# Two transformer blocks on one core: differential attention's TensorE order written out by slots of 12 products, and weights' low parts made by adding transfers

## The chip, the core and the metric

The kernel runs on one core of a Trainium2 chip. The core has five engines with an instruction queue each, which is worked off in order: TensorE (matmuls, PE in the rows, its weight loads PEld), VectorE (DVE), ScalarE (ACT), GpSimd (POOL) and SyncE (SP, which here only issues transfers). The metric is the device time of one execution in microseconds (us); the median of several executions counts.

## The reference

Two transformer blocks run one after the other on a sequence of 1024 tokens of width 1024, all in float32. The change touches one stage of the second block, differential attention, with the products that stand beside it:

```python
proj = rms_norm(x) @ w_in                       # d_q, d_k, d_v, c_val, c_gate, m_diff, m_conv, ...
for h in range(8):                              # heads: two score maps each, head width 64, values 128
    s[t] = q[h, t] @ k[h, t].T * 64 ** -0.5     # t = 0, 1; masked by chunks of 64 tokens
    pd = softmax(s[0]) - lam * softmax(s[1])
    o[h] = rms_norm(pd @ v[h], g) * (1 - lambda_init)
y_diff = sigmoid(m_diff) * o
u = c_val * sigmoid(c_gate)                     # convolution module: causal, depthwise, 31 taps
u = depthwise_conv(u, conv_dw)
```

## The kernel before

Activations lie with channels on the 128 partitions and the 1024 tokens along the free axis, in two halves of 512. A float32 product is made of three products in a rounded format (fp32r): every operand is split into a high part and the rest, its low part, and `mm3` adds high by high, high by low and low by high. So one output tile of 128 x 512 over 1024 input channels is 8 x 3 = 24 matmuls (`pdn` in the rows, line 396). A weight block of 128 x 1024 is loaded to `raw` by SP, ScalarE rounds it to `whi` (line 378), and in this stage GpSimd computes `wlo = raw - whi` (line 379, `w_conv` with `w_eng = nc.gpsimd`). For other weights the kernel has another way, `split_dma`: ScalarE writes `whi` and then `-whi` to the low part's place, and a transfer issued by GpSimd adds `raw` to it (lines 384 to 386).

The stage is the function `diff`. For each of the 8 heads, `qkv` makes keys (dk), queries (dq) and values (dv) by dense products; transfers copy the halves of k and swap those of q (`qa<-swp` is the last of that swap); `scores(qb)` makes two score maps for a block of 128 queries (`psc`), VectorE takes the row maxima (`nm`), ScalarE the exponentials (`e`), VectorE joins the two maps (line 1136); `trans` transposes them on TensorE (`ptr`), ScalarE and VectorE split them (`th`, `tl`); `pv` multiplies by the values (`po`). `finish` normalizes a head's output: `colsum` on TensorE (`pst`), a chain of short VectorE operations on 8 columns (`ms`, `rv`, `rr`, `rt`, with a root on ScalarE), a broadcast `bc`, four transposes per half (`prow`), and the products on VectorE. Beside the heads' steps, dense products for the gate (md), and for the convolution's inputs of the next head (cg, cv) fill TensorE. The convolution itself is 31 steps over a tile of 128 x 1024 for each head: one on ScalarE and 30 on VectorE (`cacc`, line 1042). They are given to the scheduler in twos and threes with a priority lowered by `LATER` = 400, to run when VectorE has nothing else.

In this stage a scheduler (of the tile framework) orders all engines, by priorities and by its own estimate of when an operand is ready. The order it makes is fixed when the program is built. On the chip each queue is worked off in that order, and an instruction that waits holds up all that stand behind it on its engine. PSUM, where TensorE writes, is given out in three pools: `psA` (2 score maps), `psB` (2 banks for `pdn`, `po`, `pst`) and `psT` (2 banks for transposes).

Of the kernel before, what the change touches and what calls it, by code (L numbers as in the profile page):

```python
# [50 lines left out]
CS = (2, 3)  # L51
# [8 lines left out]
LATE_AT = ("dk", 0)  # L60
# [225 lines left out]
class Net:  # L286
# [6 lines left out]
    def setup(self, ctx):  # L293
# [30 lines left out]
        self.w_eng = None  # L324
        self.ahead = 1
# [663 lines left out]
    def diff(self, hl, st, pre):  # L989
        nc, tc = self.nc, self.tc  # L990
# [18 lines left out]
        def dense(key, half, w):  # L1009
            ps = self.psB.tile([P, H], F32, tag="B", name="pdn")  # L1010
            self.proj_half(ps, w, hl, half)
            return ps

        def fills(h):

            st_ = {}
            cw = lambda k: self.v("conv_dw", k * CT + h)

            def fill(key, half):
                hs = slice(half * H, half * H + H)  # L1020
                if h == 0:
                    ps = pre.fills[key, half]
                else:
                    if half == 0:
                        st_[key] = self.w_next(f"{key}{h}")
                    ps = dense(key, half, st_[key])
                if key == "cg":
                    if half == 0:
                        st_["sg"] = op.tile([P, S], F32, tag="sg", name="csg")
                    nc.scalar.activation(st_["sg"][:, hs], ps, AF.Sigmoid)  # L1030
                elif key == "cv":
                    if half == 0:
                        st_["u"] = cp.tile([P, 30 + S], F32, tag="u", name="cu", bufs=2)
                        nc.gpsimd.memset(st_["u"][:, 0:30], 0.0)
                    nc.vector.tensor_tensor(st_["u"][:, 30 + half * H:30 + half * H + H],
                                            ps, st_["sg"][:, hs], op=ALU.mult)
                    if half == 1:
                        u = st_["u"]
                        acc = cp.tile([P, S], F32, tag="acc", name="cacc", bufs=1)
                        conv.append(lambda: nc.scalar.activation(acc, u[:, 30:30 + S], AF.Copy, scale=cw(30)))  # L1040
                        for k in range(30):
                            conv.append(lambda k=k: nc.vector.scalar_tensor_tensor(  # L1042
                                acc, u[:, k:k + S], cw(k), acc, op0=ALU.mult, op1=ALU.add))
                        conv.append(lambda: nc.gpsimd.dma_start(self.cvd[h], acc))
                else:
                    if half == 0:
                        st_["sig"] = op.tile([P, S], F32, tag="sig", name="sig")
                    nc.scalar.activation(st_["sig"][:, hs], ps, AF.Sigmoid)

            return st_, {k: [lambda k=k, x=x: fill(k, x) for x in range(2)] for k in ("cg", "cv", "md")}  # L1050

        def gates(i):

            x = []

            def f(half):
                if half == 0:
                    x.extend((self.w_next(f"mc{i}"),
                              cp.tile([P, 30 + S], F32, tag="u", name="mcu", bufs=2)[:, 0:S] if i % 2 else
                              op.tile([P, S], F32, tag="sg", name="mcs")))  # L1060
                w, t = x
                nc.scalar.activation(t[:, half * H:half * H + H], dense("mc", half, w), AF.Sigmoid)
                if half:
                    nc.sync.dma_start(self.sgd[i], t)

            return [lambda: f(0), lambda: f(1)]

        def ktiles():
            return [qp.tile([P, S], F32R, tag=t, name=t) for t in ("k0h", "k0l", "k1h", "k1l")]

        def qkv(h, late):

            k0h, k0l, k1h, k1l = k0 if h == 0 else ktiles()
            a = qp.tile([P, S], F32R, tag="qa", name="qa")
            b = qp.tile([P, S], F32R, tag="qb", name="qb")
            vf = op.tile([P, S], F32, tag="sg", name="vf")
            for key in ("dk", "dq", "dv"):
                w = pre.w[key] if (key, h) == ("dk", 0) else self.w_next(f"{key}{h}")
                for half in range(2):
                    if (key, h, half) == ("dk", 0, 0):  # L1080
                        continue
                    hs = slice(half * H, half * H + H)
                    ps = dense(key, half, w)
                    if key == "dk":
                        self.split(k0h[:, hs], k0l[:, hs], ps)
                    elif key == "dq":
                        nc.scalar.activation(a[:, hs], ps, AF.Copy, scale=0.125)
                        nc.vector.scalar_tensor_tensor(b[:, hs], ps, 0.125, a[:, hs].bitcast(F32),  # L1088
                                                       op0=ALU.mult, op1=ALU.subtract)
                    else:  # L1090
                        nc.scalar.copy(vf[:, hs], ps)
                    if h or key != "dk":
                        conv_steps(CS[0])
                    if (key, half) == LATE_AT:
                        for f in late:
                            f()
                if key == "dk":
                    for src, dst in ((k0h, k1h), (k0l, k1l)):
                        sf, df = src.bitcast(F32), dst.bitcast(F32)
                        nc.sync.dma_start(df[0:64, :], sf[64:128, :])  # L1100
                        nc.sync.dma_start(df[64:128, :], sf[64:128, :])
                        nc.sync.dma_start(sf[64:128, :], sf[0:64, :])
                elif key == "dq":
                    tmp = ep.tile([P, S], F32, tag="e0", name="swp")
                    swap_q(a, b, tmp)
            vh = qp.tile([P, 8, P], F32R, tag="vh", name="vh")
            vl = qp.tile([P, 8, P], F32R, tag="vl", name="vl")
            for c in range(2):
                pt = self.psT.tile([P, 4, P], F32, tag="T", name="pvt")
                for t in range(4):  # L1110
                    nc.tensor.transpose(pt[:, t, :], vf[:, (4 * c + t) * P:(4 * c + t + 1) * P], self.ident)
                self.split(vh[:, 4 * c:4 * c + 4, :], vl[:, 4 * c:4 * c + 4, :], pt)
            return (a, b), ((k0h, k0l), (k1h, k1l)), (vh, vl)

        def scores(qb, q, k, fac):
# [22 lines left out]
            return es[0]  # L1138

        def trans(qb, p, pts):  # L1140
            b = qb % 2
            n = qb + 1
            bs = slice(b * P, (b + 1) * P)
            for c in range(0, n, 4):
                w = min(4, n - c)
                ps = self.psT.tile([P, 4, P], F32, tag="T", name="ptr")
                for k in range(w):
                    nc.tensor.transpose(ps[:, k, :], p[:, (c + k) * P:(c + k + 1) * P], self.ident)
                if pts.get((c // 4)) is None:
                    pts[c // 4] = (tp.tile([P, 4, 256], F32R, tag="th", name="th", bufs=3),  # L1150
                                   tp.tile([P, 4, 256], F32R, tag="tl", name="tl", bufs=3))
                th, tl = pts[c // 4]
                self.split(th[:, 0:w, bs], tl[:, 0:w, bs], ps[:, 0:w, :])

        def pv(i, pts, v, o):
            po = self.psB.tile([P, H], F32, tag="B", name="po")
            n = 2 * i + 2
            for k in range(n):
                th, tl = pts[k // 4]
                cs = slice(P, 256) if k == n - 1 else slice(0, 256)  # L1160
                for a, m in ((v[0], th), (v[0], tl), (v[1], th)):
                    first = k == 0 and a is v[0] and m is th
                    last = k == n - 1 and a is v[1]
                    nc.tensor.matmul(po[:, cs], a[:, k, :], m[:, k % 4, cs], start=first, stop=last,
                                     skip_group_check=True)
            nc.scalar.copy(o[:, i * 256:(i + 1) * 256], po[:, 0:256])

        def finish(h, o, sig, fac):
            pst = self.psB.tile([P, H], F32, tag="B", name="pst")
# [1689 lines left out]
```

## Time and profile before

| | |
|---|---|
| median of 3 runs | 3594.99 us (3591.3 to 3597.71) |
| the profiled execution: own time, span | 3603.38 us, 3601.6 us |
| the stage looked at: from 1360 to 2172 us of the span | 812 us |
| mean granted TensorE clock, whole span | 0.96 of full |

Times on a row are microseconds from the start of the span, unless marked ns. "Idle before, releaser" is the time in which an engine stood still before an instruction, and the instruction whose end let it go on. A matmul's own duration holds the pipeline's filling; what counts for the rate is the distance between two starts.

### The profile page before, as it was taken

The page shows a single profiled execution, that of the slowest core. Times are in us where ns is not written, and L with a number is a line of the kernel's source. Part 1 is how long each engine was busy: PE and PEld are TensorE (multiplying, and loading weights), DVE is VectorE, ACT ScalarE, POOL GpSimd, SP SyncE. Part 2 cuts the span into 40 slices and gives each one's busy share as a digit, 9 for nine tenths or more (in the row PEclk, how much of TensorE's full clock was granted, in tenths as well). Part 3 has the DMA queues.
Part 4 walks back from the last instruction along what each step waited for, and adds up shares of the span by engine and source line. Part 5 has one row for each costly group of instructions (what it writes and reads, how often), then busy time and mean ns, then how long its engine had stood idle before and what let it go on. Part 6 is the DMA issues. An engine that isn't in the chain of part 4 may idle for free. (4 is left out here: it accounts for less than half of the span.)

```text
span 3601.6 us, 42275 instructions
## 1 busy us (share of the span) xinstructions
PE 3326.7 (92%) x15494; PEld 2722.3 (76%) x15494; DVE 2485.1 (69%) x3102; ACT 1673.1 (46%) x2783; POOL 1709.3 (47%) x1147
## 2 busy tenths in 40 slices
PE   8788997999998988999999999999999989999996
PEld 6668885788877776777787886777777768888775
DVE  7888838776767788888877765766477672222777
ACT  5447823444445644444444453535533233333564
POOL 3435207999952342111111126876544187776224
PEclk9889998999999989999999999999999999999998
DMA  3131231222258842222222222333455412222974
GB/s 111 38 105 51 59 117 40 86 83 83 81 178 201 208 114 73 68 73 62 68 68 66 62 67 87 130 129 117 167 202 193 146 54 87 81 83 90 273 175 109
DMA packets 127808, 386.31 MB, mean 107 GB/s; under 512 B 16016, under 2 KB 16272, under 8 KB 127600
## 3 DMA queue, kind: packets, MB, share of 16 engines
q1 hardware_dynamic: 92144, 297.58, 25.3%
q0 software_dynamic: 28400, 61.12, 8.1%
q10 hardware_dynamic: 7056, 24.91, 1.8%
q8 instruction: 122, 2.00, 0.2%
q14 instruction: 86, 0.70, 0.1%
HBM read 232.25 MB, written 84.97 MB: 88 GB/s over the span
## 5 line engine op out<-in xcount | busy, mean ns | idle before, releaser
L379 POOL TENSOR_TENSOR wlo<-raw,whi 128x512 fp32r<-128x512 f32 (+1 forms) x266 | 478.0, 1808 | 788.8 <-ACT whi L378 771.9
L396 PE MATMUL pdn<-h,whi 128*128 128x512 f32 x1664 | 534.4, 402 | 16.8 <-DVE qb L1088 7.3
L1542 DVE TENSOR_TENSOR f<-pf,f 128x512 f32<-128x512 f32 x224 | 154.0, 688 | 363.2 <-PE pf L396 362.7
L378 ACT CAST whi<-raw 128x512 fp32r<-128x512 f32 (+1 forms) x283 | 206.7, 753 | 387.9 <-PE pf L396 169.1
L396 PEld LDWEIGHTS pdn<-h,whi 128*128 128x128 f32 x1664 | 314.6, 193 | 83.1 <-DVE qb L1088 10.2
L1042 DVE SCALAR_TENSOR_TENSOR cacc<-cu,vec,cacc 128x1024 f32<-128x1024 f32 x240 | 357.9, 1491 | 9.8 <-issue 2.2
L396 PE MATMUL pdn<-h,wlo 128*128 128x512 f32 x832 | 331.4, 398 | 0.0
L396 PE MATMUL pd<-whi 128*128 128x512 f32 x644 | 257.8, 400 | 22.1 <-DVE f L1542 10.8
L396 PE MATMUL pd<-whi,wlo 128*128 128x512 f32 x644 | 258.8, 402 | 14.6 <-DMA wlo<-fs 10.2
L396 PE MATMUL pd<-wlo,whi 128*128 128x512 f32 x644 | 256.2, 398 | 0.0
L378 ACT CAST whi<-sb 128x512 fp32r<-128x512 f32 x128 | 79.1, 620 | 342.2 <-PE pf L396 253.7
L379 POOL TENSOR_TENSOR wlo<-sb,whi 128x512 fp32r<-128x512 f32 x128 | 174.3, 1366 | 108.7 <-ACT whi L378 108.5
L379 POOL TENSOR_TENSOR wlo<-sa,whi 128x1024 fp32r<-128x1024 f32 x64 | 178.4, 2788 | 55.5 <-ACT whi L378 55.3
L396 PE MATMUL pf<-h,whi 128*128 128x512 f32 x576 | 183.8, 401 | 10.6 <-ACT a L2469 5.6
L396 PEld LDWEIGHTS pdn<-h,wlo 128*128 128x128 f32 x832 | 160.2, 193 | 33.9
L396 PE MATMUL pp<-h,whi 128*128 128x512 f32 x448 | 149.3, 413 | 24.3 <-ACT h L532 10.1
L386 POOL DMA_DIRECT2D wlo<-fs x92 | 79.9, 871 | 192.8 <-ACT wlo L385 138.8
L396 PEld LDWEIGHTS pd<-whi 128*128 128x128 f32 x644 | 124.2, 193 | 51.5 <-ACT acc L1875 7.9
L396 PEld LDWEIGHTS pd<-whi,wlo 128*128 128x128 f32 x644 | 124.3, 193 | 50.5 <-DMA wlo<-fs 15.9
L396 PEld LDWEIGHTS pd<-wlo,whi 128*128 128x128 f32 x644 | 124.1, 193 | 26.2
L396 PEld LDWEIGHTS pf<-h,whi 128*128 128x128 f32 x576 | 109.4, 192 | 37.9 <-ACT a L2469 6.0
L1542 DVE TENSOR_TENSOR g<-pf,g 128x512 f32<-128x512 f32 x93 | 63.4, 686 | 105.4 <-PE pf L396 89.6
(563 smaller groups left out, 9576.8 us busy)
## 6 DMA issues: line engine op xcount, KB each, us to landing
raw<-in_w_in_dram SPq DMA_DIRECT2D x102, 512.0 KB, 3.5
raw<-in_w_up_dram SPq DMA_DIRECT2D x48, 512.0 KB, 3.5
gd<-f ACTq DMA_DIRECT2D x46, 512.0 KB, 2.6
fs<-gd SPq DMA_DIRECT2D x46, 512.0 KB, 7.0
wlo<-fs POOLq DMA_DIRECT2D x92, 256.0 KB, 5.0
raw<-in_w_ffn_in_dram SPq DMA_DIRECT2D x44, 512.0 KB, 3.5
wlo<-s POOLq DMA_DIRECT2D x69, 256.0 KB, 3.9
fs<-in_w_down_dram SPq DMA_DIRECT2D x24, 512.0 KB, 6.4
```

The costliest lines, as they stand in the source:

```text
L378: (copy or self.nc.scalar.copy)(hi, src)
L379: (eng or self.nc.vector).tensor_tensor(lo, src, hi.bitcast(F32), op=ALU.subtract)
L386: nc.gpsimd.dma_start(lo.bitcast(F32), src, accum_op=ALU.add)
L396: nc.tensor.matmul(out, a, b, start=(first and i == 0), stop=(last and i == n - 1), skip_group_check=cont)
L1042: conv.append(lambda k=k: nc.vector.scalar_tensor_tensor(acc, u[:, k:k + S], cw(k), acc, op0=ALU.mult, op1=ALU.add))
L1542: e.tensor_tensor(o, x, y, op=op)
```

## The change

Three things are changed in `diff`.

1. TensorE's order in the stage is no longer the scheduler's: it is the order in which the code issues (`tc.manual_schedule(engines={nc.tensor.engine})`). The dense products are run by `run(blocks)` in slots of 12 (half of a tile of 24). After each slot, the steps of attention that `plan` has put down for that slot's number are issued. A head has 24 slots (blocks dv, md, cg, cv, dk, dq of four slots each; the first head 20, without md). In a head's own count, values are transposed after slots 3 and 5, scores of query block qb stand after slot 4 + 2 qb, their transposes 3 slots later, `pv` of a pair of blocks 5 slots after the second's scores, and the normalization after slots 25 (`norm_sums`), 27 and 28 (`norm_rows`), which are slots 1, 3 and 4 of the next head. The first and the last head have a closer pace (1.5 and 1.7 slots for a block in place of 2).
2. `po` and `pst` lie in `psT`, no longer in `psB`. The next head's keys and queries are made at the end of a head, not at the beginning of its own.
3. `w_dma` is on in the stage: low parts of the weights come from `split_dma` in place of GpSimd's subtraction, on 48 blocks of 128 x 1024 and one of 128 x 128.

VectorE, ScalarE, GpSimd and SP keep the scheduler's order, which is another one, since it is made for the new order of TensorE. The convolution steps are given two after each slot.

```diff
     def w_conv(self):
         ...
-        self.split(hi, lo, raw, self.w_eng)
+        if self.w_dma:
+            self.split_dma(hi, lo, raw)
+        else:
+            self.split(hi, lo, raw, self.w_eng)
     def diff(self, hl, st, pre):
         ...
         def pv(h, i):
-            po = self.psB.tile([P, H], F32, tag="B", name="po")
+            po = self.psT.tile([P, H], F32, tag="T", name="po")
         ...
-        def finish(h, o, sig, fac):
-            pst = self.psB.tile([P, H], F32, tag="B", name="pst")
+        def norm_sums(h):
+            pst = self.psT.tile([P, H], F32, tag="T", name="pst")
             ...
+        def norm_rows(h, half):
             ...
+        def plan(h, base, pace):
+            s = [base + 4 + round(pace * qb) for qb in range(8)]
+            for c in range(2):
+                at(base + 3 + 2 * c, values, h, c)
+            for qb in range(8):
+                at(s[qb], scores, h, qb)
+                at(s[qb] + 3, trans, h, qb)
+                if qb % 2:
+                    at(s[qb] + 5, pv, h, qb // 2)
+            at(s[7] + 7, norm_sums, h)
+            at(s[7] + 9, norm_rows, h, 0)
+            at(s[7] + 10, norm_rows, h, 1)
+        def run(blocks):
+            for key, i in blocks:
+                if (key, i) not in wts:
+                    wts[key, i] = self.w_next(f"{key}{i}")
+                for half in ((1,) if (key, i) == ("dk", 0) else (0, 1)):
+                    ps = self.psB.tile([P, H], F32, tag="B", name="pdn")
+                    for k in (0, CT // 2):
+                        self.proj_half(ps, wts[key, i], hl, half, range(k, k + CT // 2), k == 0, k > 0)
+                        if k:
+                            evac[key](i, half, ps)
+                        if self.slot >= 0:
+                            self.slot += 1
+                            for f in events.pop(self.slot, ()):
+                                f()
+                            conv_steps(2)
         ...
-        for h in range(8):
-            q, k, v = qkv(h, late)
-            if done:
-                finish(*done)
-            ...
-            ps_ = [scores(qb, q, k, fac) for qb in range(2)]
-            ...
-            for qb in range(8):
-                ...
-                trans(qb, ps_.pop(0), pts)
-                if qb + 2 < 8:
-                    ps_.append(scores(qb + 2, q, k, fac))
-                if todo:
-                    todo.pop(0)()
-                conv_steps(CS[1])
-                if qb % 2:
-                    pv(qb // 2, pts, v, o)
-                    pts = {}
-            done = (h, o, st_["sig"], fac)
+        self.w_dma = True
+        with tc.manual_schedule(engines={nc.tensor.engine}):
+            self.slot = -1
+            run([("dk", 0), ("dq", 0)])
+            self.slot = 0
+            base = 0
+            for h in range(8):
+                blocks = [("dv", h)] + [("md", h)] * (h > 0)
+                blocks += ([(k, h + 1) for k in ("cg", "cv", "dk", "dq")] if h < 7 else
+                           [("mc", i) for i in range(MC)])
+                plan(h, base, (1.5 if h == 0 else 1.7) if h in (0, 7) else 2)
+                run(blocks)
+                base += 4 * len(blocks)
+            for x in sorted(events):
+                for f in events[x]:
+                    f()
```

How the program's order moves is seen at one place that comes back at each change from head to head. On TensorE before, at the fourth head's start, sums of squares of the old head (`pst`), the new head's values (`pvt`) and its first scores (`psc`) stand close together:

```order
L1111 MATMUL pvt<-ident,vf 128x128 x4
L434 MATMUL pst<-onef,osq 128x1 x4
L1111 MATMUL pvt<-ident,vf 128x128 x4
L396 MATMUL pdn<-h_0_10262,whi 128x512 x2
L396 MATMUL pdn<-h_0_10262,wlo 128x512
L434 MATMUL pst<-onef,osq 128x1 x4
L1123 MATMUL psc<-k0h,qa 128x128
L1124 MATMUL psc<-k0l,qa 128x128
L1123 MATMUL psc<-k1h,qb 128x128
L1124 MATMUL psc<-k1l,qb 128x128
L396 MATMUL pdn<-h_1_10284,whi 128x512 x2
```

The normalization's `prow` stood 26 dense products further on, mixed into the third block's scores. TensorE now, at the same change of heads, 24 dense products (two slots) after the 8 of `pst`:

```order
L452 MATMUL prow<-ident,bc 128x128 x4
L1098 MATMUL pvt<-ident,vf 128x128 x4
L398 MATMUL pdn<-h_4_10507,whi 128x512 x2
L398 MATMUL pdn<-h_4_10507,wlo 128x512
L398 MATMUL pdn<-h_5_10508,whi 128x512 x2
L398 MATMUL pdn<-h_5_10508,wlo 128x512
L398 MATMUL pdn<-h_6_10509,whi 128x512 x2
L398 MATMUL pdn<-h_6_10509,wlo 128x512
L398 MATMUL pdn<-h_7_10510,whi 128x512 x2
L398 MATMUL pdn<-h_7_10510,wlo 128x512
L452 MATMUL prow<-ident,bc 128x128 x4
L1115 MATMUL psc<-k0h,qa 128x128
```

The old head's normalization now stands ahead of the new head's first scores, with fixed numbers of dense products between its steps: 24 from `pst` to the first `prow`, 12 to the second.

On VectorE before, from the queries' low part (`qb`) on, at the same place:

```order
L1088 SCALAR_TENSOR_TENSOR qb<-pdn,qa 128x512
L1042 SCALAR_TENSOR_TENSOR cacc<-cu,vec,cacc 128x1024 x5
L1088 SCALAR_TENSOR_TENSOR qb<-pdn,qa 128x512
L1042 SCALAR_TENSOR_TENSOR cacc<-cu,vec,cacc 128x1024 x8
L379 TENSOR_TENSOR vl<-pvt,vh 128x512 x2
L1176 TENSOR_TENSOR ms<-pst,fac 128x8
L1127 TENSOR_REDUCE nm<-psc 128x1
L1177 TENSOR_TENSOR ms<-ms,fac 128x8
L1127 TENSOR_REDUCE nm<-psc 128x1
L418 TENSOR_SCALAR rv<-ms 128x8
L1042 SCALAR_TENSOR_TENSOR cacc<-cu,vec,cacc 128x1024
```

VectorE now, from `qb` to the first short operations of the normalization:

```order
L1075 SCALAR_TENSOR_TENSOR qb<-pdn,qa 128x512
L1036 SCALAR_TENSOR_TENSOR cacc<-cu,vec,cacc 128x1024 x6
L1075 SCALAR_TENSOR_TENSOR qb<-pdn,qa 128x512
L1036 SCALAR_TENSOR_TENSOR cacc<-cu,vec,cacc 128x1024 x2
L1173 TENSOR_TENSOR ms<-pst,fac 128x8
L1036 SCALAR_TENSOR_TENSOR cacc<-cu,vec,cacc 128x1024
L1174 TENSOR_TENSOR ms<-ms,fac 128x8
L1036 SCALAR_TENSOR_TENSOR cacc<-cu,vec,cacc 128x1024
L420 TENSOR_SCALAR rv<-ms 128x8
```

and straight on, to the broadcast that `prow` reads:

```order
L1036 SCALAR_TENSOR_TENSOR cacc<-cu,vec,cacc 128x1024 x2
L423 RECIPROCAL rr<-rr 128x8
L1036 SCALAR_TENSOR_TENSOR cacc<-cu,vec,cacc 128x1024
L425 SCALAR_TENSOR_TENSOR rt<-rv,rr 128x8
L1036 SCALAR_TENSOR_TENSOR cacc<-cu,vec,cacc 128x1024
L426 TENSOR_TENSOR rt<-rt,rr 128x8
L1036 SCALAR_TENSOR_TENSOR cacc<-cu,vec,cacc 128x1024
L427 SCALAR_TENSOR_TENSOR rr<-rt,rr 128x8
L1036 SCALAR_TENSOR_TENSOR cacc<-cu,vec,cacc 128x1024
L1176 SCALAR_TENSOR_TENSOR rr<-rr,fac 128x8
L1036 SCALAR_TENSOR_TENSOR cacc<-cu,vec,cacc 128x1024
L443 COPY bc<-rr 128x512
```

The run of eight convolution steps ahead of `vl` is gone; nine steps now stand one by one (once two) between the first `ms`, which reads `pst`, and the `bc` that the first `prow` transposes. Each of the heads' changes has the same nine. From the end of slot 16, where the convolution's input of the next head is complete (`cu`, line 1035), to that `bc`, 27 of the 30 steps of a convolution stand in VectorE's queue.

## Rows read from the trace of the kernel before

**Rows 1.** The page, part 1: busy time, share of the span and instructions of each engine.

```profile
PE 3326.7 (92%) x15494; PEld 2722.3 (76%) x15494; DVE 2485.1 (69%) x3102; ACT 1673.1 (46%) x2783; POOL 1709.3 (47%) x1147
```

**Rows 2.** Stretches: us; busy (count) of PE, PEld, DVE, ACT, POOL; PE clock; DMA.

```profile
1360.00:2172.00 812.00, 760.10 (x3786) 633.43 (x3785) 637.49 (x846) 388.69 (x773) 150.30 (x79) 0.97 0.24 68
...
1800.00:1850.00 50.00, 50.00 (x261) 42.53 (x260) 29.95 (x51) 32.25 (x66) 8.46 (x6) 0.99 0.15 53
1850.00:1900.00 50.00, 45.14 (x210) 36.79 (x209) 49.32 (x57) 14.60 (x30) 8.92 (x4) 0.90 0.33 79
```

**Rows 3.** Waits of TensorE in the stage: us in total, times, longest.

```profile
PE psc L1123 <- ACT e L1130: 18.3, 7, 3.4
PE pdn L396 <- DVE k0l L379: 6.9, 1, 6.9
```

**Rows 4.** Timeline, TensorE: start, us, instruction, [idle before it and releaser].

```profile
1409.71 0.33 PE L1123 MATMUL psc<-k0h,qa 128*128 128x128 f32 x1 [0.57 <-DMA qa<-swp]
...
1499.79 0.30 PE L1123 MATMUL psc<-k0h,qa 128*128 128x128 f32 x1 [0.59 <-DMA qa<-swp]
...
2088.24 0.47 PE L1123 MATMUL psc<-k0h,qa 128*128 128x128 f32 x1 [1.80 <-DMA qa<-swp]
...
2171.37 7.56 PE L2455 MATMUL pf<-h,wf 128*32 128x512 f32 x32
```

**Rows 5.** Timeline, VectorE: the stage's start, then the fourth head's.

```profile
1376.57 11.02 DVE L1042 SCALAR_TENSOR_TENSOR cacc<-cu,vec,cacc 128x1024 f32<-128x1024 f32 x6 [1.88 <-ACT cacc L1040]
...
1683.28 12.51 DVE L1042 SCALAR_TENSOR_TENSOR cacc<-cu,vec,cacc 128x1024 f32<-128x1024 f32 x8
...
1697.52 1.27 DVE L1042 SCALAR_TENSOR_TENSOR cacc<-cu,vec,cacc 128x1024 f32<-128x1024 f32 x1
...
1698.83 1.28 DVE L1042 SCALAR_TENSOR_TENSOR cacc<-cu,vec,cacc 128x1024 f32<-128x1024 f32 x1
```

**Rows 6.** Groups of the stage: instruction, count | busy us, mean ns | idle before.

```profile
L1042 DVE SCALAR_TENSOR_TENSOR cacc<-cu,vec,cacc 128x1024 f32<-128x1024 f32 x240 | 357.9, 1491 | 9.8 <-issue 2.2 <-ACT cacc L1040 1.9
L379 POOL TENSOR_TENSOR wlo<-raw,whi 128x1024 fp32r<-128x1024 f32 (+2 forms) x51 | 132.5, 2600 | 525.8 <-ACT whi L378 510.6 <-DMA k0l<-k0l 15.2
L1040 ACT ACTIVATE cacc<-cu,vec 128x1024 f32<-128x1024 f32 x8 | 9.3, 1162 | 0.0
L379 DVE TENSOR_TENSOR tl<-ptr,th 128x512 fp32r<-128x512 f32 x48 | 32.2, 684 | 45.9 <-ACT th L378 45.9
L1127 DVE TENSOR_REDUCE nm<-psc 128x1 f32<-128x1024 f32 x16 | 18.8, 1210 | 1.5 <-ACT psc L1125 1.5
L1136 DVE SCALAR_TENSOR_TENSOR e<-e,sm 128x1024 f32<-128x1024 f32 x8 | 10.2, 1277 | 0.0
```

**Rows 7.** Timeline, TensorE: dense products, then a block of attention's.

```profile
1723.26 0.61 PE L396 MATMUL pdn<-h,whi 128*128 128x512 f32 x2
...
1723.94 0.61 PE L396 MATMUL pdn<-h,whi 128*128 128x512 f32 x2
...
1742.26 0.48 PE L1123 MATMUL psc<-k0h,qa 128*128 128x512 f32 x1
...
1744.19 0.28 PE L1164 MATMUL po<-th,vh 128*128 128x256 f32 x1
...
1746.27 0.95 PE L1148 MATMUL ptr<-ident,e 128*128 128x128 f32 x7
```

**Rows 8.** Stretches around two changes of the clock (columns as in Rows 2).

```profile
1388.00:1392.00 4.00, 3.75 (x10) 2.98 (x11) 3.93 (x5) 0.00 (x0) 0.00 (x0) 0.57 0.69 131
1392.00:1394.00 2.00, 2.00 (x11) 1.64 (x10) 1.97 (x4) 0.00 (x0) 0.00 (x0) 1.00 0.93 264
...
1791.00:1801.00 10.00, 8.54 (x23) 6.66 (x24) 9.96 (x23) 5.27 (x15) 0.41 (x1) 0.50 0.15 53
```

**Rows 9.** The line of transfers that add (feed-forward weights): ns min/median/max.

```profile
L386 POOL DMA_DIRECT2D wlo<-fs x92: 847/870/1136, 1045.1 to 3553.2; - x92
DMA to landing us min/median/max: 3.2/4.4/8.8
```

More of the change, by code (lines that the diff above doesn't have):

```diff
@@ L324, in setup @@
         self.w_eng = None
+        self.w_dma = False
         self.ahead = 1
@@ L1052, in gates @@
[L1052 to L1113, printed above, removed]
@@ new lines, in evac_dk @@
+        def evac_dk(h, half, ps):
+            x = heads[h]
+            if half == 0:
+                x.k = [qp.tile([P, S], F32R, tag=t, name=t) for t in ("k0h", "k0l", "k1h", "k1l")]
+            k0h, k0l, k1h, k1l = x.k
+            self.split(k0h[:, hs_(half)], k0l[:, hs_(half)], ps)
+            if half:
+                for src, dst in ((k0h, k1h), (k0l, k1l)):
+                    sf, df = src.bitcast(F32), dst.bitcast(F32)
+                    nc.sync.dma_start(df[0:64, :], sf[64:128, :])
+                    nc.sync.dma_start(df[64:128, :], sf[64:128, :])
+                    nc.sync.dma_start(sf[64:128, :], sf[0:64, :])
@@ new lines, in evac_dv, with values @@
+        def evac_dv(h, half, ps):
+            x = heads[h]
+            if half == 0:
+                x.vf = op.tile([P, S], F32, tag="sg", name="vf")
+            nc.scalar.copy(x.vf[:, hs_(half)], ps)
+        evac = {"cg": evac_cg, "cv": evac_cv, "md": evac_md, "mc": evac_mc, "dk": evac_dk, "dq": evac_dq,
+                "dv": evac_dv}
+        mcs, wts = {}, {}
+        def values(h, c):
+            x = heads[h]
+            if c == 0:
+                x.vh = qp.tile([P, 8, P], F32R, tag="vh", name="vh")
+                x.vl = qp.tile([P, 8, P], F32R, tag="vl", name="vl")
+            pt = self.psT.tile([P, 4, P], F32, tag="T", name="pvt")
+            for t in range(4):
+                nc.tensor.transpose(pt[:, t, :], x.vf[:, (4 * c + t) * P:(4 * c + t + 1) * P], self.ident)
+            self.split(x.vh[:, 4 * c:4 * c + 4, :], x.vl[:, 4 * c:4 * c + 4, :], pt)
@@ L1116, in scores @@
+        def scores(h, qb):
+            x = heads[h]
+            if qb == 0:
+                x.fac = op.tile([P, 8], F32, tag="fac", name="fac", bufs=2)
+                x.o = op.tile([P, S], F32, tag="o", name="o")
+                x.e, x.pts = {}, {}
+            q, k, fac = (x.a, x.b), (x.k[0:2], x.k[2:4]), x.fac
             nk = (qb + 1) * P
@@ new lines, in norm_rows @@
+        def norm_rows(h, half):
+            x, hs = heads[h], hs_(half)
+            pb = self.psT.tile([P, H], F32, tag="T", name="prow")
+            self.bcast_rows(pb, x.r[:, half * 4:half * 4 + 4], op, "bc", 1)
+            nc.vector.scalar_tensor_tensor(x.o[:, hs], x.o[:, hs], self.v("diff_ng", 0), pb,
+                                           op0=ALU.mult, op1=ALU.mult)
+            if half:
+                nc.vector.tensor_tensor(x.o, x.o, x.sig, op=ALU.mult)
+                nc.gpsimd.dma_start(self.yd[h], x.o)
@@ L1234, in diff @@
-        for f in more[4:5] + late + more[5:6]:
-            f()
-        finish(*done)
-        for f in more[6:]:
-            f()
+        self.w_dma = True
[14 more added lines that the diff above has]
+                    f()
```

171 lines of the change are left out of this document (79 added, 92 removed).

## The prediction

> **What bounds the kernel now.** The page's first part comes first: TensorE is busy for 92% of the span, no other engine above 76% [rows 1]. So a change pays only where TensorE stands still or runs at the lower of its two clock levels, and the reader looks for such places in the stage that is rewritten. In its 812 us TensorE is busy for 760, at a mean granted clock of 0.97 [rows 2]. 52 us stand still; another 24 (3% of 812) are lost by the lower level. No rewriting of the order alone can win more than these 76 us.
>
> Next, when do they fall? Two neighbouring stretches show it. From 1800 to 1850 TensorE is busy throughout at 0.99; from 1850 to 1900 it is busy for 45 of 50 us at 0.90, and there VectorE is busy for 49.3 of 50 [rows 2]. Heads repeat: from the second head's first scores to the eighth's there are 588.45 us, 98.1 per head [rows 4]. The waits name VectorE's work or ScalarE's that stands behind it: scores for the exponentials 18.3 us in 7 waits, up to 3.4 each, and products for a low part 6.9 once [rows 3]. At a change of heads VectorE works off eight convolution steps in one run, 12.51 us [rows 5], ahead of the values' split and the row maxima; the second block's scores wait for the exponentials behind them.
>
> **What TensorE needs per head.** Three dense products take 0.68 us (1723.26 to 1723.94), so a slot of 12 takes 2.73 and 24 slots 65.5 [rows 7]. Attention's part: scores of eight products of 512 columns take 1.93 (1742.26 to 1744.19), 0.24 each; 24 such, and 24 shorter ones at about 0.14, make 9. The 18 products of `po` take 2.08, so 60 take 7. The 52 transposes take 0.1 each, 5. The sums `pst` take 1.7 and the changes between kinds of work 1.5 (estimates from the same stretch). Together 89.5, so a head loses 8.6 us now.
>
> **The change part by part.**
>
> *Low parts by transfers.* GpSimd loses its subtractions (132.5 us) and issues 49 transfers at 0.87: 43 us [rows 6, 9]. Its queue was not on the path. ScalarE gains 48 passes over 128 x 1024. The nearest row is its convolution step, 1.16 us [rows 6]: 56 us on an engine busy for 389 of 812 [rows 2]. Hidden by ScalarE's idle time, except at the stage's start (below). The first step's gain is VectorE's: beside subtractions a convolution step took 1.84 (six in 11.02), without them steps start 1.31 apart when chained (1697.52 to 1698.83, a short operation in between) and 1.20 when other work follows [rows 5]. Mean 1.49 against 1.28 over 240 steps is 50 us of VectorE, 6 per head [rows 5, 6].
>
> *The order by slots.* Waits inside a head should go: transposes now follow their scores by three slots, 8.2 us, where the chain is two maxima, two exponentials and one join (1.21 x 2 + 1.3 x 2 + 1.28 = 6.3 for the longest block) [rows 6, 7]. `po` in `psT` waits for a copy at most some tenths.
>
> *The change of heads.* Here the order makes a new wait. I count from the end of slot 16, when the next convolution's input is complete, to the `bc` that the first `prow` needs. VectorE has in that stretch: 27 convolution steps at 1.20, plus 9 direct neighbours at 0.11 more, 33.4; four maxima (two of 896 columns at 1.1, two of 1024 at 1.2) 4.4; two joins 2.3; six splits 3.2; two low parts of keys and two of queries 2.4; the short operations and `bc` 1.8 [rows 5, 6]. Sum 47.5. Ahead of the first step lie 0.7 for the input and 1.16 for ScalarE's first step, with hand-overs 2.0, and I allow 0.5 for gaps: 50.0. TensorE in the same stretch: slots 17 to 27, 30.0; scores 3.7; transposes 2.0; `po` 4.9; `pst` 1.7; changes 0.7: 43.0 [rows 7]. So it arrives at `prow` 7.0 us early and stands. Nothing behind `prow` can pass it: the new head's values, its first scores and all dense products are queued there. It can't be shorter than the part after `pst`: nine steps at 1.31 and the short operations are 12.2 us, against two slots, 5.5.
>
> The other part of a head is TensorE's own, since no convolution step stands there: 13 slots 35.5, scores of six blocks 5.5, `po` 2.0, transposes 3.0, changes 1.0: 47.0. ScalarE has about 6.5 us of work for each two slots (7 us) there, with two table loads; hidden, but without much room.
>
> *The clock.* After the wait of 6.9 us TensorE worked for four microseconds at a mean 0.57 and then at 1.00 [rows 8]: 1.7 lost. I take 1.6 per change of heads. The other bound is the change at 1791 to 1801: ten microseconds at 0.50, the 1.2 GHz level, 4.3 lost of 8.5 busy [rows 8].
>
> So a middle head takes 47.0 + 50.0 + 1.6 = 98.6 against 98.1: six of them, **+3**.
>
> *Start and first head.* Before, 1409.71 to 1499.79 [rows 4], with 6.9 of waiting ahead of it [rows 3]. Now three steps, not six, stand ahead of the keys' low part: 3.9 in place of 11.0 [rows 5]; but ScalarE has three more passes ahead, 3.5, and the first weight's low part comes by a transfer with no lead. That leaves 3.6 of 6.9 won. In the first head 57 steps of two convolutions run with 20 slots; VectorE's work, about 104 us, is longer than TensorE's, and I count 5 to 10 us of gaps. Its end then falls 5 us earlier to 1 later than now: I take **-2**, bounds -8 and +3.
>
> *Last head and end.* No convolution is left. Before, first scores to the next stage took 83.1 (2088.24 to 2171.37) [rows 4]. Now 20 slots 54.6, attention 22, a wait of 1.5 for the last normalization, some tenths: 79. **-4**, bounds -6 and 0 (the last output's store is now at the very end).
>
> Sum: +3 - 2 - 4 = -3 us on 3603.4 of the profiled execution. The median shown is 8.4 lower; I take the same step from it and round the small waits that I have not counted up by one: **3593 us**, within 0.2% (7 us), which is about what a measurement of this kernel tells from no change.
>
> **The rivals.**
>
> *A. The wait is there, but low ends hold* (33%, with the next). VectorE's run without gaps (49.5), the first head bound by TensorE's side, and a change of clock that costs 1 us: middle heads 97.0 to 97.5, -5, the start -7, the end -5: about 3578. For it: VectorE's durations are well known [rows 5, 6]. Against: gaps are only ever added. *B. No wait at `prow` at all*, as the order would have it: heads of 89.5, seven times -8.6 and -4: 3531. It would need VectorE to have finished its nine steps in two slots, which 12.2 against 5.5 excludes; 3 of the 33.
>
> *C. Slower: the standstill takes the clock down for long* (22%). One mechanism: after a standstill of 7 us at every change of heads, the lower level lasts for ten microseconds as at 1791, not four. Price 2.7 to 3.6 more per change, seven changes: +19 to +25, 3615. It decides once more than 2.5 us per change are lost. For it: the present changes of heads lose about 4 us each by the clock. Against: there, work trickled with gaps, while now full slots follow [rows 8].
>
> *D. Slower: low parts come late* (7%). Place: a slot's second product reads `wlo`. The transfers seen carry 256 KB and land in 4.4 us at the median, 8.8 at most [rows 9]; twice the size at twice the time is 17.6 as an upper estimate. Conversions stand two to three blocks ahead in ScalarE's queue, some 20 to 33 us, which covers it. Without that cover each block would wait up to 10 us. A tenth of the 48 late by 5 us is +24: 3618. On GpSimd itself the issues seen took 0.85 to 1.14 us, 0.87 at the median, while VectorE worked [rows 9]; all 48 at the longest would be 13 us more, spread over 812 us of a queue with idle time, so the sum stands.
>
> The Trainium skill, page SBUF — State Buffer, section "SBUF: two separate sides", speaks against such transfers: GpSimd can't write the descriptors of a transfer that it issues while VectorE runs an operation that uses both of its ports on one tensor, and the transfer stands still so long. No row here shows such a hold. By that rule D would be likelier than the issue times make it; by the issue times its price is the 13 us, and uncovered they would give 3606.
>
> *E. The change comes to nothing* (38%): the forecast; one standstill is exchanged for another of nearly the same length. Own range 3587 to 3601.
>
> **Numbers.** Faster than 3587.8: A and B, 0.33. Within 0.2%: 0.38. Slower than 3602.2: C and D, 0.29. The range takes in most of A and C: 3574 to 3614.
>
> **What would show it.** In the profile after: TensorE's waits led by `prow` for VectorE's `bc`, seven times, 6 to 8 us each; the waits for exponentials nearly gone; convolution steps at a mean of 1.23 to 1.30; head to head 97.5 to 99.5; clock near 0.5 for some 3 us after each `prow`. It is wrong if `prow` waits under 4 us (then faster, A), or if products wait for `wlo` (D).

## The result and the profile after

The changed kernel takes 3620.46 us (median of 4 runs, 3617.57 to 3624.74) beside 3593.14 us (4 runs, 3588.79 to 3597.71): a ratio of 1.0077, 95% interval 1.0059 to 1.0094. It is slower by 27 us, which the forecast of 3593 and its range to 3614 didn't hold. The profiled execution took 3619.3 us, its span is 3617.5.

The stretches of the changed kernel, each from a head's first scores to the next's: the start, the first, second, fifth, sixth and last head, and all that follows the stage (columns as in [rows 2]):

```profile
1317.00:1412.00 95.00, 74.86 (x315) 60.72 (x313) 64.36 (x85) 36.90 (x53) 19.01 (x18) 0.88 0.50 123
1412.00:1513.30 101.30, 89.33 (x416) 73.85 (x417) 81.95 (x112) 45.28 (x92) 4.85 (x8) 0.89 0.32 79
1513.30:1615.80 102.50, 95.48 (x468) 80.28 (x466) 72.05 (x104) 55.22 (x103) 6.46 (x9) 0.93 0.38 90
...
1814.50:1913.60 99.10, 91.53 (x467) 77.19 (x465) 72.01 (x104) 55.10 (x103) 6.29 (x10) 0.97 0.41 99
1913.60:2012.60 99.00, 91.42 (x467) 77.15 (x466) 72.02 (x104) 55.13 (x103) 6.37 (x9) 0.97 0.40 99
2111.70:2194.30 82.60, 80.08 (x415) 67.73 (x413) 38.03 (x76) 55.91 (x104) 14.31 (x13) 0.98 0.25 75
2194.30:3617.50 1423.20, 1322.62 (x5935) 1067.27 (x5932) 825.65 (x1087) 594.85 (x955) 819.72 (x591) 0.96 0.42 134
```

The same cuts in the kernel before: the start, the first head, and what follows the stage:

```profile
1319.00:1409.70 90.70, 77.29 (x328) 62.66 (x326) 71.13 (x84) 31.96 (x48) 29.23 (x18) 0.91 0.32 93
1409.70:1499.80 90.10, 80.52 (x404) 66.04 (x404) 84.17 (x99) 40.45 (x87) 15.99 (x8) 0.98 0.23 62
...
2171.40:3601.60 1430.20, 1326.67 (x5933) 1071.43 (x5931) 824.65 (x1085) 595.82 (x956) 819.85 (x590) 0.96 0.42 134
```

Start and first head: 196.3 in place of 180.8. The six middle heads: 598.4 (1513.3 to 2111.7) in place of 588.45 [rows 4]. The last head: 82.6 in place of 83.1. The stretch behind, where no line was changed: 7 less. With 2 us less ahead of the stage the spans differ by 16, the medians by 27; what lies between is the step from one execution to a median (below).

TensorE's waits in the stage of the changed kernel (columns as in [rows 3]):

```profile
PE prow L452 <- DVE bc L443: 46.7, 7, 6.9
PE psc L1115 <- DMA qa<-swp: 11.7, 1, 11.7
PE pst L436 <- ACT osq L1168: 5.8, 8, 0.8
PE psc L1115 <- ACT e L1122: 3.9, 2, 2.2
PE pdn L398 <- DVE k0l L381: 2.6, 1, 2.6
```

The waits for exponentials fell from 18.3 [rows 3] to 3.9. In their place stand seven waits at `prow`, and one of 11.7 for the first swapped queries. Why `prow` waits is read from VectorE's timeline at the fifth head's start, here from the sums to the first broadcast:

```profile
1796.40 0.17 DVE L1173 TENSOR_TENSOR ms<-pst,fac 128x8 f32<-128x8 f32 x1 [0.73 <-PE pst L436]
1796.49 1.28 DVE L1036 SCALAR_TENSOR_TENSOR cacc<-cu,vec,cacc 128x1024 f32<-128x1024 f32 x1
...
1799.12 2.61 DVE L1036 SCALAR_TENSOR_TENSOR cacc<-cu,vec,cacc 128x1024 f32<-128x1024 f32 x2
...
1807.05 1.28 DVE L1036 SCALAR_TENSOR_TENSOR cacc<-cu,vec,cacc 128x1024 f32<-128x1024 f32 x1
1808.25 0.42 DVE L443 COPY bc<-rr 128x512 f32<-128x512 f32 x1
```

Nine convolution steps stand between short operations of a sixth of a microsecond each: 11.85 us from the sums to the start of `bc`. TensorE had worked off its two slots by 1801.97 and took `prow` up at 1808.81:

```profile
1808.81 1.09 PE L452 MATMUL prow<-ident,bc 128*128 128x128 f32 x4 [6.84 <-DVE bc L443]
```

### The profile page after: what moved, and what is told of

Same layout as the page of the kernel before. It is cut to its first block, busy times and chain, and to the rows that moved or that the text cites. A ratio compares the mean times of both kernels' runs of the same rounds, so it can differ in the third digit from the quotient of the medians.

```text
span 3617.5 us, 42471 instructions
## 1 busy us (share of the span) xinstructions
PE 3323.9 (92%) x15494; PEld 2723.6 (75%) x15494; DVE 2432.3 (67%) x3102; ACT 1738.6 (48%) x2846; POOL 1623.0 (45%) x1147
## 3 DMA queue, kind: packets, MB, share of 16 engines
q0 software_dynamic: 35456, 86.35, 11.9%
## 5 line engine op out<-in xcount | busy, mean ns | idle before, releaser
L381 POOL TENSOR_TENSOR wlo<-raw,whi 128x512 fp32r<-128x512 f32 (+1 forms) x217 | 347.6, 1614 | 273.1 <-ACT whi L380 271.3
L1036 DVE SCALAR_TENSOR_TENSOR cacc<-cu,vec,cacc 128x1024 f32<-128x1024 f32 x240 | 307.2, 1280 | 17.2 <-ACT cacc L1034 14.3
L388 POOL DMA_DIRECT2D wlo<-raw x49 | 42.4, 865 | 569.0 <-ACT wlo L387 511.9
L380 ACT CAST whi<-raw 128x512 fp32r<-128x512 f32 (+1 forms) x234 | 156.0, 694 | 231.4 <-PE pf L398 169.2
L387 ACT ACTIVATE wlo<-whi 128x512 fp32r<-128x512 f32 (+2 forms) x210 | 152.8, 728 | 5.2
L1119 DVE TENSOR_REDUCE nm<-psc 128x1 f32<-128x256 f32 (+7 forms) x128 | 91.1, 751 | 77.4 <-ACT psc L1117 77.0
```

The lines of the kernel that those rows point to most:

```text
L380: (copy or self.nc.scalar.copy)(hi, src)
L381: (eng or self.nc.vector).tensor_tensor(lo, src, hi.bitcast(F32), op=ALU.subtract)
L387: nc.scalar.activation(lo, hi.bitcast(F32), AF.Copy, scale=-1.0)
L388: nc.gpsimd.dma_start(lo.bitcast(F32), src, accum_op=ALU.add)
L1036: conv.append(lambda k=k: nc.vector.scalar_tensor_tensor(acc, u[:, k:k + S], cw(k), acc, op0=ALU.mult, op1=ALU.add))
L1119: nc.vector.tensor_reduce(nm, ps[:, 0:nk], axis=mybir.AxisListType.X, op=ALU.max, negate=True)
```

## The experiments

Times are medians; a ratio is to the kernel before, timed on the same chip. The runs were timed on several chips, where the kernel before took 3593.1 to 3599.4 us, so runs of different chips are compared by their ratios.

| run | median us | ratio, 95% interval |
|---|---|---|
| the change | 3620.46 | 1.0077, 1.0059 to 1.0094 |
| order alone | 3643.13 | 1.0135, 1.0120 to 1.0151 |
| transfers alone | 3590.94 | 0.9990, 0.9980 to 0.9999 |
| change, rows 3 slots later | 3587.07 | 0.9973, 0.9965 to 0.9982 |
| change, gate's block later | 3587.18 | 0.9965, 0.9953 to 0.9977 |
| that, first head's attention later | 3578.49 | 0.9944, 0.9932 to 0.9956 |
| that, rows 1 slot later | 3583.96 | 0.9956, 0.9942 to 0.9970 |
| that, swap on GpSimd | 3560.97 | 0.9902, 0.9885 to 0.9919 |
| or that, loads on GpSimd | 3564.49 | 0.9903, 0.9885 to 0.9921 |
| transfers alone, swap on GpSimd | 3563.02 | 0.9907, 0.9890 to 0.9924 |
| change, swap on GpSimd | 3607.84 | 1.0035, 1.0021 to 1.0048 |
| change, half the steps (work left out) | 3564.58 | 0.9904, 0.9890 to 0.9918 |

**The kernel before, profiled again.** No edit.

> The kernel before once more, unchanged, for a second profile. If the lower clock at the changes to heads 5 to 8 (10 us at 0.5 each in the first profile, heads of 98.0 to 99.9 us there against 96.3 and 96.5 for heads 2 and 3) was that execution's own, heads 5 to 8 come back here at 96 to 97 us and the time near 3593. If it belongs to the kernel, the same heads are 98 to 100 us long again.

3605.39 us, beside a median of 3596.47 (21 runs, 3588.83 to 3604.4). A head of its middle, at a clock of 0.97:

```profile
1595.80:1695.00 99.20, 93.11 (x466) 77.93 (x466) 78.09 (x105) 46.62 (x94) 17.36 (x10) 0.97 0.24 67
```

Heads 3 to 7 took 98.7 to 99.9 (first scores to first scores). So long heads at a lower clock were no accident of the first profile; but both profiled executions lie 9 to 10 us over their medians, and no profile of a median execution is at hand.

**The order alone.**

```diff
         st.enter_context(self.psum(2, 2, 2))
-        self.w_dma = True
         with tc.manual_schedule(engines={nc.tensor.engine}):
```

> The order by slots as changed, but the weights' low parts by GpSimd's subtractions as before. Theory 1 (the standstill at the broadcast rows makes the loss; the adding transfers only crowd the start): convolution steps beside subtractions get longer again (mean 1.4 to 1.5 us), the wait at prow grows from 6.8 to 8 or 9 us, middle heads take 100 to 102; the wait of 11.7 for the swapped queries shrinks to 4 or 5; in all 3615 to 3630. Theory 2 (the adding transfers are what costs): the wait at prow stays, but heads and start are shorter by what the transfers take, 3595 or less.

3643, over the upper end of theory 1. Its waits and its convolution steps in the stage (the groups' columns as in [rows 6]):

```profile
PE prow L452 <- DVE bc L443: 68.0, 7, 10.3
PE psc L1115 <- DMA qa<-swp: 2.8, 1, 2.8
```
```profile
L1036 DVE SCALAR_TENSOR_TENSOR cacc<-cu,vec,cacc 128x1024 f32<-128x1024 f32 x226 | 324.1, 1434 | 10.7 <-ACT cacc L1034 8.0
L381 POOL TENSOR_TENSOR wlo<-raw,whi 128x1024 fp32r<-128x1024 f32 (+2 forms) x46 | 106.9, 2324 | 493.8 <-ACT whi L380 490.4 <-PE psc L1116 3.4
```

The order is what costs. Here, too, nine convolution steps stand between the sums and `bc`, and VectorE takes the same 11.9 us for them; the fifth head's start:

```profile
1806.10 0.16 DVE L1173 TENSOR_TENSOR ms<-pst,fac 128x8 f32<-128x8 f32 x1
...
1817.99 0.42 DVE L443 COPY bc<-rr 128x512 f32<-128x512 f32 x1
```
```profile
1818.56 1.09 PE L452 MATMUL prow<-ident,bc 128*128 128x128 f32 x4 [10.30 <-DVE bc L443]
```

But TensorE had made the sums by 1802.65, and VectorE, still at earlier and longer steps, read them 3.5 us later. So the wait is longer, 9.7 on average: VectorE is late for the whole stretch, not only behind the sums. The adding transfers shorten a step from 1434 ns to 1280 and so win part of it back. But with them the first swap waits 11.7, without them 2.8.

**The transfers alone**, in the order of the scheduler (with the branch in `w_conv`, as in the change).

```diff
+        self.w_dma = True
         for h in range(8):
             q, k, v = qkv(h, late)
```

> The kernel before with the low parts by adding transfers in the stage, its order made by the scheduler as before. Theory 1: VectorE wins 50 us over the stage, and since the change of heads in that order waits for VectorE's run of convolution steps, heads get 2 to 4 us shorter: 3565 to 3582. Theory 2: the transfers crowd the copies of keys and the swap of queries, which in that order stand directly ahead of each head's first scores; those wait 3 to 8 us longer per head: 3610 to 3640.

3591, between the two: 5 us faster, just clear of noise. Both mechanisms are there. Steps fell to 1281 ns, and the scores wait for swapped queries instead, 3.5 us in all before:

```profile
PE psc L1127 <- DMA qa<-swp: 34.1, 8, 9.7
PE pdn L400 <- DVE k0l L383: 7.8, 7, 2.6
```

**The broadcast rows three slots later.**

```diff
-            at(s[7] + 9, norm_rows, h, 0)
-            at(s[7] + 10, norm_rows, h, 1)
+            at(s[7] + 12, norm_rows, h, 0)
+            at(s[7] + 13, norm_rows, h, 1)
```

> The changed kernel with the broadcast rows of the normalization three slots (8.2 us) later, after slots 6 and 7 of the next head instead of 3 and 4. Theory 1 (TensorE is early at prow by 6.8 us and nothing else holds it): the waits at prow fall below 0.5 us, the lower clock after them goes, heads take 91 to 92.5 in place of 99.1: 3562 to 3575. Rival (VectorE is the bound of the whole stretch, so the lag only moves): transposes, scores or products wait for VectorE behind it, heads stay at 96 to 99, 3600 or more.

3587: 33 us come back, more than the change had lost, but not the 45 to 58 that theory 1 gave. The waits:

```profile
PE pdn L398 <- ACT sig L1044: 13.9, 6, 2.8
PE psc L1115 <- DMA qa<-swp: 11.8, 1, 11.8
PE prow L452 <- DVE bc L443: 1.3, 1, 1.3
```

`prow` no longer waits in the heads. A wait that neither theory had takes part of its place: dense products wait for ScalarE to empty the gate's PSUM into `sig`. Both halves of that work stand in ScalarE's queue together, behind the old head's output, which reads the one buffer of `sig` (at the fourth head's start `o<-o,sig` ended at 1703.98), a weight's conversion and the loading of a function table (1.28 us), and began at 1705.65. That the shared buffer set this order is read from the code, not tested.

**The gate's block later.** In heads 2 to 7 the convolution's input is complete four slots earlier, and the gate's products come further behind the old head's output. The list of the weights follows the same order.

```diff
-                blocks = [("dv", h)] + [("md", h)] * (h > 0)
-                blocks += ([(k, h + 1) for k in ("cg", "cv", "dk", "dq")] if h < 7 else
-                           [("mc", i) for i in range(MC)])
+                md = [("md", h)] * (h > 0)
+                blocks = [("dv", h)] + ([("cg", h + 1), ("cv", h + 1)] + md + [("dk", h + 1), ("dq", h + 1)]
+                                        if h < 7 else md + [("mc", i) for i in range(MC)])
         ...
```

> The changed kernel with the gate's block (md) moved behind the convolution's two blocks (cg, cv) in heads 2 to 7, so that the convolution's input is complete four slots earlier; the broadcast rows stand where the change put them. Theory 1 (VectorE has more work between the convolution's input and bc, 50 us, than TensorE until prow, 43): TensorE gets about 13 us more in that stretch, VectorE three steps and about 4 us of attention; four steps are left between the sums and bc, about 7 us against two slots of 5.5; the wait falls from 6.8 to 2 us or less for six heads, heads take 93 to 94.5: 3578 to 3592. Rival (the chain from the sums to bc with its hand-overs sets the wait, whatever stands ahead of it): the wait stays at 5 us or more, 3608 to 3620.

3587, as theory 1 had it, with middle heads of 94.2 to 94.7. Of its waits at `prow` one is the first head's, 6.2, where nothing was moved; seven share the other 7.9:

```profile
PE psc L1115 <- DMA qa<-swp: 15.1, 5, 11.7
PE prow L452 <- DVE bc L443: 14.1, 8, 6.2
```

**The first head's attention two slots later, on top.**

```diff
-                plan(h, base, (1.5 if h == 0 else 1.7) if h in (0, 7) else 2)
+                plan(h, base + 2 * (h == 0), (1.5 if h == 0 else 1.7) if h in (0, 7) else 2)
```

> The run with the gate's block later, and the first head's steps of attention all two slots later. Theory 1 (the start lost 11.7 us to the swap of the first queries, which the adding transfers slow): two slots of products, 5.5 us, cover half of that wait; 3 to 8 us faster than the run with the gate's block later alone. Rival (what the start wins the first head's VectorE loses again behind it): within 2 us of it.

3578, 9 us less: theory 1, a little over its range. The start's wait for the swap fell to 6.9, the first `prow` to at most 2.8:

```profile
PE prow L452 <- DVE bc L443: 10.5, 8, 2.8
PE psc L1115 <- DMA qa<-swp: 9.3, 3, 6.9
```

**The rows one slot later, on top** (`s[7] + 10` and `s[7] + 11`).

> The run before with the broadcast rows one slot later (2.73 us), which covers what is left of the wait at prow. Theory 1: no wait over 0.5 us at prow, and the lower clock behind it goes: heads 90.5 to 92.5, 3560 to 3575, faster than both kernels. Rival (a later prow delays the old head's output and so the tiles that the new head writes): waits for the gate's sigmoid or the copies of po take its place, no gain over the run before.

3584, no gain over the run before that shows (the two intervals overlap), as the rival said, but by another wait than those it named; what `prow` gives up, 8.8 us, the swapped queries take, 9.4:

```profile
PE psc L1115 <- DMA qa<-swp: 18.7, 7, 6.9
PE prow L452 <- DVE bc L443: 1.7, 2, 1.3
```

The profiled execution took 3574.6, 9 under the median of its runs, and that of the run before 3583.1, 5 over. SP's queue at the change to its fifth head, and GpSimd's beside it:

```profile
1764.21 0.46 SPq L1008 DMA_DIRECT2D swp<-qb  x1
1771.79 0.33 SPq L353 DMA_DIRECT2D raw<-in_w_in_dram  x1
1772.21 0.46 SPq L1009 DMA_DIRECT2D qb<-qa  x1
1777.52 0.46 SPq L1010 DMA_DIRECT2D qa<-swp  x1
```
```profile
1764.00 0.86 POOL L388 DMA_DIRECT2D wlo<-raw  x1 [13.81 <-ACT wlo L387]
```

`swp` landed at 1767.56, but `qb<-qa` was issued at 1772.21. Between them in SP's queue stands a weight load that needs the buffer `raw`, and the adding transfer of 1764.00 read that buffer until 1771.72. In the changed kernel the last transfer of the same swap was issued at 1801.58, while TensorE stood still at `prow` until 1808.81, so no scores waited for it. Loads waited on SP's queue in the kernel before as well, there for GpSimd's subtractions (462.2 us in 40 waits).

**The swaps on GpSimd's queue; the weight loads there instead; the swaps with the transfers alone; the swaps in the changed kernel.** Four runs, with these two edits:

```diff
-            nc.sync.dma_start(tmp[64:128, :], bf[0:64, :])
+            nc.gpsimd.dma_start(tmp[64:128, :], bf[0:64, :])
             ...
-            self.nc.sync.dma_start(raw, ap)
+            (self.nc.gpsimd if self.w_dma else self.nc.sync).dma_start(raw, ap)
```

> The run with gate and rows later, and the three transfers that swap a head's queries issued by GpSimd instead of SP. Theory 1 (a weight's load stands between them in SP's queue and waits there until an adding transfer has let its buffer go; the swap waits behind it): the waits for the swapped queries, 18.7 us in 7 there, fall to 6 us or less; 8 to 12 us faster than that run. Theory 2 (the transfers themselves get longer beside the adding ones, whichever queue issues them): the waits stay at 12 us or more, and the time within 4 us.

> The run with gate and rows later; the swaps stay with SP, and the stage's weight loads are issued by GpSimd, so that nothing on SP's queue waits for an adding transfer. Theory 1: the waits for the swapped queries fall to 6 us or less; 8 to 12 us faster than that run, unless loads that GpSimd holds up make products wait for their weights. Theory 2: they stay at 12 us or more.

> The kernel before with the adding transfers alone, and the swaps issued by GpSimd. Theory 1 (SP's queue): the waits for the swapped queries, 34.1 us in 8 in the run with the transfers alone, fall to 12 us or less, and the time to 3562 to 3578. Theory 2 (longer transfers): they stay at 25 us or more, 3585 to 3597.

> The changed kernel with nothing altered but the queue of the swaps, GpSimd in place of SP. Theory 1 (the start's wait of 11.7 us for the swapped queries comes from SP's queue, and the standstills at prow are another loss that this does not touch): the start wins 4 to 8 us, seven waits at prow of 6 to 7 us stay, 3609 to 3617. Rival (VectorE's two convolutions bound the first head, so an earlier start only waits longer at the first prow): that wait grows by what the start wins, 3617 to 3624.

The waits for swapped queries, in this order of the runs:

```profile
PE psc L1115 <- DMA qa<-swp: 6.2, 3, 4.0
```
```profile
PE psc L1115 <- DMA qa<-swp: 5.8, 4, 4.5
```
```profile
PE psc L1127 <- DMA qa<-swp: 17.3, 8, 7.9
```
```profile
PE psc L1115 <- DMA qa<-swp: 9.6, 1, 9.6
PE prow L452 <- DVE bc L443: 48.9, 8, 6.9
```

3561 and 3564: both beat both kernels, and whichever of the two kinds of transfers leaves SP, the waits of 18.7 fall to 6: theory 1. The gain by the medians, 19 us (0.9956 against 0.9902 and 0.9903), is larger than the 8 to 12 forecast; between the profiled executions it is 8 to 10.

With the transfers alone the time, 3563, is theory 1's; the waits, 17.3, lie between the two theories (in an execution of 3571.9, 9 over the median). So about half of the 34 us went with SP's queue. The rest goes with longer transfers: those to and from `swp` landed 4.5 us after their issue at the median, 2.9 before. That GpSimd's queue has no part in the rest was not tested, and neither was the swaps' queue in the kernel before without adding transfers, where scores waited 3.5 us for them.

In the changed kernel the swaps' queue is worth 13 us by the medians, 15 by the ratios and 10 between the profiles: theory 1's time, a little better. Its mechanism holds only in part. Of the start's wait of 11.7, 9.6 stay, so most of that wait is not the queue's. The first scores come 3.5 us earlier, and the first and second heads get 4.2 and 3.4 shorter, at mean clocks of 0.92 and 0.97 in place of 0.89 and 0.93. The waits at `prow` stay, the first at 6.6 in place of 6.2, so the rival, that the first `prow` eats the gain, falls.

**Half the convolution steps.** Each head's convolution is left half done, 15 of 30 steps on VectorE.

```diff
-                for k in range(30):
+                for k in range(15, 30):
```

> The changed kernel without 15 of each head's 30 convolution steps on VectorE (work is left out, the convolution is not complete). Theory 1 (VectorE's work sets the wait): the wait at prow falls to 1 us or less, since no step is left between the sums and bc; heads 91 to 92.5: 3560 to 3575. Rival (the hand-overs between TensorE, VectorE and ScalarE in the normalization are too long for two slots): the wait stays at 4 us or more, 3600 or more.

3565, theory 1. Every middle head takes 92.1, and the first 86.3 in place of 101.3:

```profile
PE psc L1115 <- DMA qa<-swp: 12.1, 1, 12.1
...
PE prow L452 <- DVE bc L443: 2.0, 2, 1.3
```
```profile
1774.80:1866.90 92.10, 91.37 (x467) 77.18 (x466) 54.32 (x89) 55.18 (x103) 6.45 (x9) 0.98 0.44 106
```

## Why the prediction was wrong

**Right: the standstill and a head's length.** Of the steps, the change of heads held best: 7.0 us forecast at `prow`, 6.84 measured. VectorE's stretch from the end of slot 16 to `bc` was put at 50.0 us; at the fifth head's start it runs from 1758.08 to 1808.67 (`bc` above), 50.6, and TensorE's until it stands at `prow` 43.9, forecast 43.0:

```profile
1758.28 0.69 DVE L1030 TENSOR_TENSOR cu<-pdn,csg 128x512 f32<-128x512 f32 x1 [1.12 <-PE pdn L398]
```

That this work sets the wait is shown from both sides, by the gate's block (more room, wait nearly gone) and by half the steps (less work, wait gone). TensorE's own need was put at 89.5 (its two parts by place, 43.0 and 47.0, make 90.0); with half the steps a head takes 92.1, of which 0.7 is a standstill at `pst` and some 1.7 goes to the lower clock (a mean of 0.98): 89.7. A head with the standstill was to take 98.6; the last four middle heads take 99.0 to 99.2. The clock's 1.6 per change is 1.7 there (99.0 less 89.7 and 7.6 of standing still), so rival C's ten microseconds at each head fall for these changes; the first two lost more (below). Convolution steps at 1.28 us, the waits for exponentials, and low parts that nobody waits for (no product waits for `wlo`) came as written.

**Wrong: "Start and first head", -2.** It is the term that failed: +15.5 (196.3 against 180.8), 4.3 of it in the start, 11.2 in the first head. I won 4.3 at the keys' low part (6.9 [rows 3] to 2.6; 3.6 were costed), but gave the adding transfers no price on other transfers. The copies of keys and the swap stand on SP's queue with the weight loads. The DMA engines are busy for 0.50 of the start in place of 0.32; `swp` landed 8.0 us after its issue where 4.0 was the longest before; and the first scores waited 11.7. Taking the swaps off SP's queue gave back 10 to 15 us of the whole loss, though only 2.1 of the 11.7.

For the first head I allowed 5 to 10 us of gaps for the two convolutions. It stood still for 12.0, but before it had stood still for 9.6; more was lost by the lower clock, which I had not counted there. TensorE is busy for 89.3 us at a mean clock of 0.89. With half the steps it is busy with as many products for 82.9 at 0.96, and the head is 15 us shorter. From 1412 to 1416, behind the wait for the swap, the clock was at 0.50, the 1.2 GHz level. It was near that level again from the sums `pst` on, ahead of the standstill, at the ends of the first head and of the second:

```profile
1490.00:1499.00 9.00, 8.28 (x27) 6.78 (x28) 6.43 (x8) 1.85 (x3) 0.16 (x1) 0.62 0.73 177
1594.00:1602.00 8.00, 8.00 (x25) 6.50 (x25) 5.28 (x7) 1.76 (x2) 0.00 (x0) 0.58 0.79 189
```

That is some 3 us lost at each (an estimate: busy time times what the clock lacks). Why it fell there and not at the later changes is not shown.

**Wrong in part: the middle heads, +3, were +9.9.** Four of six hit; the first of them took 102.5, at a clock of 0.93. With the swaps on GpSimd all six take 99.0, so that tail goes with the swaps' queue; by what way is not shown.

**Wrong in size: "Last head and end", -4.** It gained 0.5. Attention there took some 24.5 by difference (82.6 less 54.6 of products, 2.5 of standing still and 1 for the clock), where I put 22.

**Wrong: "I take the same step from it".** The profiled execution of before lay 10 us above the median of its runs, that of the changed kernel 1 below. So 11 of the 27 us are in no row of the two profiles. The second profile of before lies as high, at heads of 99 us and a lower clock at their changes. In what a median execution differs stays open; a loss of clock at some changes of heads would suit it, but that is only argued. Executions without a profile go with it: of the 11 of the kernel before that were timed beside the three runs of 3561 to 3564, the three shortest (3590 to 3591) had mean clocks of 0.962 to 0.965, the three longest (3602 to 3606) 0.956 to 0.959.

**Open.** Behind the stage all runs with an edit shown above take 1422 to 1427 us, both profiles of before 1430 and 1428, though TensorE's order there is the same in the changed kernel as in before. The cause was not looked for.

**Rivals.** None of the four as written was the outcome. C's price, 2.7 to 3.6 more, was met at two of seven changes, but by a lower level that began ahead of the standstill. Its "about 4 us each" for the changes before is too high for some: the second and third heads before stood at a clock of 1.00. D named the adding transfers, at another place: not the low parts were late, but the transfers beside and behind them; and on the whole those transfers gain, since the same order without them takes 3643.

On the page of the Trainium skill that was weighed there (SBUF — State Buffer, "SBUF: two separate sides"), the trace shows no such hold: the 49 issues on GpSimd (minimum, median and longest below, of the changed kernel) took 861 to 885 ns, with VectorE busy for 72 of 99 us. More than half of that are convolution steps, which read two tensors; whether an operation of the kind that the page names ran beside an issue is not shown.

```profile
L388 POOL DMA_DIRECT2D wlo<-raw x49: 861/863/885, 1369.1 to 2143.5; - x49
...
DMA to landing us min/median/max: 2.4/4.6/8.7
```

## What to carry to other kernels

An order written by hand must be laid against every engine that feeds it: count the slow engine's work between the input that it needs and the product that waits for it, and put that product later or the input earlier, before the order is fixed. When an operation on a busy engine is replaced by transfers, cost them on the neighbours as well: which buffers they hold longer, what waits for those buffers on an in-order queue, and what stands behind it. Here the transfers with the swaps on another queue, in the scheduler's own order, gave as much (0.9907) as the repaired order by hand (0.9902).

## What the runs showed of the hardware

The transfers to and from `swp` (64 x 1024, 256 KB) landed 2.9 us after their issue at the median before (2.8 to 4.0 for all). In the changed kernel, beside adding transfers of 512 KB, the median was 3.0, but the first took 8.0; with the transfers alone the median was 5.1. A standstill of TensorE of 6.84 us costs more than itself, but little, at the last five changes of heads: 1.7 us through the lower clock.
